# A two-layer decoder trunk on one Trainium2 core: the first FFN pair by eight plain products, and the order of the reloads ahead of the down projection

## The chip, the cores and the metric

The kernel runs on one core of one Trainium2 chip. The metric is the device time of one execution in microseconds (us), lower is better. A core has a matrix engine (TensorE, PE in the profile, with its weight loads as PEld), a vector engine (DVE), a scalar engine (ACT), GpSimd (POOL) and a sync engine (SP) that issues most DMAs. Each engine works through its own instruction queue in order, and waits on semaphores for the others.

## The reference

A segment of a decoder over 1040 positions (16 meta tokens and 1024 tokens) of width 1024, all in float32:

```python
for layer in range(2):
    if layer == 0:
        h = h + mixer_rglru_swa(rmsnorm(h, mix_norm_ab), ...)   # recurrent heads and windowed attention
    else:
        h = h + mixer_retention(rmsnorm(h, mix_norm_ret), ...)  # chunkwise retention
    h = h + swiglu(rmsnorm(h, ffn_norm[layer]), w_gu[layer], w_down[layer])
return h[:, 16:]

def swiglu(x, w_gu, w_down):                 # w_gu (1024, 5632), w_down (2816, 1024)
    gate, up = split(x @ w_gu, 2)
    return (silu(gate) * up) @ w_down
```

The change lies in the two FFNs (`swiglu`) and in what leads into them.

## The kernel before, in words

**Numbers as two halves.** Activations lie with the 1024 features on partitions (8 tiles of 128, index `m`) and the positions along the free axis, cut into two halves (`hf` 0 and 1, each 520 positions in layer 0 and 512 in layer 1). An operand of TensorE is a pair of fp32r tiles: `hi` is a rounded copy (ACT), `lo` is the rest (a subtraction). `hilo` (line 767) makes such a pair of an activation (tiles `oh`, `ol`), `part` (line 108) of a weight (tiles `hi`, `lo`). A product of two operands is three matmuls, `mm3` (lines 149 to 151): hi by hi, lo by hi, hi by lo.

**Seven products.** The FFN's big matrix products are done on 2 by 2 blocks: two tiles of output features by two halves of positions, summed over pairs of input tiles. `seven` (line 773) does such a block with seven products in place of eight (`PRODUCTS`, line 742). For that both sides need sums and differences. The weights' four, S1 to S4, are made on POOL by `unit22` (line 125). The activations' four, T1 to T4, are made by `mixed` (line 759):

```python
t1 = b12 - b11;  t2 = b22 - t1;  t3 = b22 - b12;  t4 = b21 - t2
```

Here `b11` and `b21` are tiles 2j and 2j+1 of half 0, `b12` and `b22` the same tiles of half 1. `MOVING` (line 744) lists the seven activation operands of a block, B11, B21, T2, T1, T3, B22 and T4. `operands` (line 862) makes them for one pair of tiles `j`, with the four differences taken in turn by POOL and DVE and the seven `lo` halves by DVE. There are four such `j`.

**The up phase.** `ffn` (line 790) first runs 11 pairs (`NP`). A pair is one `seven` for the gate columns and one for the up columns, each over the four `j`. Its evacuation applies the norm's scale `R` (made by `ratio`, line 255, from the sums of squares `acc`), Silu, and the product gate by up. Then `mixed` makes the hidden block's own differences, and the seven operands of the pair are written to DRAM (`hd`, on ACT's DMA queue).

**The down phase.** It reads the 16 residual tiles back (`unspill`, line 737, tiles `h<-keep`), and then works in four groups of hidden pairs, (0, 1), (2, 3, 4), (5, 6, 7) and (8, 9, 10). For each group it reloads the seven operands of its pairs (`raw<-hd`, line 847), splits them with `hilo` (the `lo` on POOL), and runs `seven` for each of four blocks `mp` of output tiles, adding into `h` (line 801). The last group hands `h` to `done`.

**What leads into an FFN.** In layer 0 the attention's output projection `out_proj` (line 683) runs for half 0 in the background of attention, and then for half 1, tile by tile: projection, add to `h` (line 694), `normed` (line 746, tile `xp`, on DVE, with the square on ACT and its sum `acc` on POOL, line 756), spill of `h`, and after every second tile `operands`. In layer 1 the retention's last projection (line 1153) does the same, and half 0 is reloaded and normed in `prefetch` (line 1092).

**Buffers.** Pool `sl` has 56 slots of one activation tile each, got by `slot`. Pool `fp` of an FFN has 18 more (`xslot`, `fslot`, tag `xs`). Weight halves `hi` and `lo` have 6 buffers each, raw weight tiles 2, and PSUM has 4 banks of tag `ps` and 4 of tag `ax`.

**Who orders the work.** The code is traced in program order and then scheduled: each instruction gets its place in its engine's queue from a simulated timeline, by priority (program order, with weight loads raised by `tc.high_priority`), as its inputs and a free buffer come available in that simulation. On the chip the queues then run in that order.

Of the kernel before, what the change touches and what calls it, by code (L numbers as in the profile page):

```python
# [22 lines left out]
P = 128  # L23
D = 1024
KD = 8
NM = 16
# [45 lines left out]
def tile_hybrid(ctx: ExitStack, tc, hT, wfm, wqkv, wo0, lruw, pk, qkg, ck, c0, ret_tab, ret_m,  # L72
# [46 lines left out]
    def unit(src, early=True, eng=nc.vector, pool=None):  # L119
        with tc.high_priority() if early else ExitStack():  # L120
            raw = raw_tile()
            nc.sync.dma_start(raw, src)
            return [part(raw[:, i * 512:(i + 1) * 512], 512, eng, pool) for i in range(2)]

# [662 lines left out]

    NP = FT // 2

    def ffn(fp, wgu, wd, xs, R, n, done):  # L790
# [13 lines left out]
        for i in range(NP):  # L804
# [27 lines left out]
            seven(unit22(wgu[i], 512, fp), xs, chunks, blocks(gt))  # L832
            seven(unit22(wgu[NP + i], 512, fp), xs, chunks, blocks(ut))
            m_ = mixed(((ut["11"], ut["12"]), (ut["21"], ut["22"])), n, xslot, (nc.vector,))
# [4 lines left out]
        for m in range(KD):  # L839
            for hf in range(2):  # L840
                h[m][hf] = unspill(m, hf, n, xslot if hf and m >= 4 else None)
        for gi, grp in enumerate(DGROUPS):
            xs = [{} for _ in grp]
            for key in MOVING:
                for j, i in enumerate(grp):
                    raw = xslot("raw")[:, :n]
                    nc.sync.dma_start(raw, hd[i][key])
                    xs[j][key] = hilo(raw, n, slot, nc.gpsimd)
            w = len(grp) * P
            for mp in range(4):  # L850
                h1, h2 = h[2 * mp], h[2 * mp + 1]
# [10 lines left out]
    def operands(j, xp, n, temps, new, eng):  # L862

        m_ = mixed((xp[2 * j], xp[2 * j + 1]), n, temps, (nc.gpsimd, nc.vector))
        return {k: hilo(m_[k], n, new, eng) for k in MOVING}
# [12 lines left out]
    xp = [[None, None] for _ in range(KD)]  # L878
    for m in range(KD):
        xp[m][0] = normed(m, 0, "g1", 520, sc[0], acc[0])  # L880
        spill(m, 0, 0, 520)
    for m in range(KD):
# [3 lines left out]
    xo = []  # L886
    for m in range(KD):
# [4 lines left out]
        if m == 0:  # L892
            Rf = [ratio(acc[0], 520, sc[0], fp), None]
        if m % 2:
            xo.append(operands(m // 2, xp, 520, slot, fslot if m == 5 else slot, nc.vector))
    Rf[1] = ratio(acc[1], 520, sc[1], fp)
# [21 lines left out]
    ffn(fp, wgu0, wd0, xo, Rf, 520, done0)  # L918
# [6 lines left out]
    xo = []  # L925
    acc3 = [None, None]
    with tc.tile_pool(name="m1", bufs=1) as rp:
# [13 lines left out]
        for hf in range(2):  # L941
# [40 lines left out]
            for hd in range(NH):  # L982
# [109 lines left out]
                def prefetch():  # L1092
# [4 lines left out]
                    for kk in range(KD):  # L1097
# [3 lines left out]
                        else:  # L1101
                            xp[kk][0] = normed(kk, 0, "g3", 512, R[0][:, NM:528], acc3[0])

# [42 lines left out]
                def project(u, u_, a, b, yh, yl):  # L1146
                    for j in range(2):
# [8 lines left out]
                        elif b - a == 256 and b == 512:  # L1156
                            xp[m][1] = normed(m, 1, "g3", 512, R[1][:, :512], acc3[1])
                            spill(m, 1, 0, 512)
                            if m in (1, 3, 5):
                                xo.append(operands(m // 2, xp, 512, slot, slot, nc.vector))  # L1160
# [21 lines left out]
    xo.append(operands(3, xp, 512, slot, fslot, nc.vector))  # L1182
# [132 lines left out]
```

## Time and profile before

| what | us |
|---|---|
| time, median of 3 runs | 2770.39 |
| lowest and highest of these | 2769.83 and 2771.3 |
| time of the profiled execution | 2795.01 |
| span of the profiled execution, first to last instruction | 2793.2 |
| PE busy in it | 2654.5 |
| DVE busy | 1653.4 |
| POOL busy | 1381.9 |
| ACT busy | 1142.6 |

The span is what the profile's views divide up, and the profiled execution's own time stands 1.8 us above it. Matmuls are pipelined, so a busy PE is told best by how many matmuls it starts in a stretch. The granted clock of TensorE is given as a share of its full speed (1.00 or 0.5). In a row of the timeline the first two numbers are the start and the duration in us, `x2` means that rows were merged, and the brackets tell how long the engine had been idle before and what ended that. In a row of groups the mean duration in ns stands behind the busy time, and the idle time with its releasers at the end. In a row of a tile three durations in ns are given, the shortest, the median and the longest.

### The profile page before, as it was taken

To read this page: it belongs to the slowest core of one execution; us is meant where nothing else is said; L and a number is where in the kernel's file an instruction comes from. 1 tells how busy PE (TensorE), PEld (TensorE's weight loads), DVE (VectorE), ACT (ScalarE), POOL (GpSimd) and SP (SyncE) were. 2 spreads that over 40 slices of the span, in tenths; PEclk is the share of its full clock that TensorE was granted. 3 is DMA by queue.
4 is the path that set the end of the run, shared out by engine and by line. 5 is a ranking of instruction groups with operands and counts; after the bars stand their busy time and mean duration, and the time that the engine had idled before them with its cause. 6 is when DMAs were issued, how large, how long until landed. Compare 5 with 4: busy or idle time off the path is not lost.

```text
span 2793.2 us, 42909 instructions
## 1 busy us (share of the span) xinstructions
PE 2654.5 (95%) x16079; PEld 2345.8 (84%) x16079; DVE 1653.4 (59%) x2956; ACT 1142.6 (41%) x2350; POOL 1381.9 (49%) x1267
## 2 busy tenths in 40 slices
PE   8979997999999799999999999999967999997999
PEld 7867795999999799988888888888865888885787
DVE  6866458666666577734434454344386565554775
ACT  4654434333333344333434444334443333333342
POOL 3654125554555677733234243343365554555885
PEclk9989698999999899999999999999988999998999
DMA  4001032223222744222121242222231233326442
GB/s 154 32 16 37 29 137 72 84 97 114 96 95 85 262 132 134 94 74 76 69 83 64 80 143 70 91 76 76 83 113 46 102 103 105 113 76 228 152 148 90
DMA packets 111073, 274.59 MB, mean 98 GB/s; under 512 B 13520, under 2 KB 13776, under 8 KB 110864
## 3 DMA queue, kind: packets, MB, share of 16 engines
q1 hardware_dynamic: 87840, 228.86, 24.3%
q10 hardware_dynamic: 22464, 41.14, 3.9%
q8 instruction: 126, 2.06, 0.3%
q0 software_dynamic: 560, 1.85, 0.2%
q14 instruction: 83, 0.68, 0.1%
HBM read 216.37 MB, written 55.43 MB: 97 GB/s over the span
## 4 chain that ended last, share of the span: by engine, by line
PE 88%; DVE 5%; POOL 2%; ACT 2%; issue 2%; DMA 1%; SPq 0%; ACTq 0%; POOLq 0%; DVEq 0%
PE ps L149 19%; PE ps L150 19%; PE ps L151 19%; PE ax L149 8%; PE ax L150 8%; PE ax L151 8%; PE ps L659 1%; PE ps L626 1%; POOL ol L770 1%; DVE lo L113 1%; DVE ol L770 1%; PE ax L642 1%; DVE qs L280 1%; PE ax L1029 1%; PE ps L625 1%
## 5 line engine op out<-in xcount | busy, mean ns | idle before, releaser
L149 PE MATMUL ps<-oh,hi 128*128 128x260 f32 (+1 forms) x1584 | 509.8, 324 | 64.5 <-ACT oh L769 45.0
L150 PE MATMUL ps<-ol,hi 128*128 128x260 f32 (+1 forms) x1584 | 511.7, 324 | 32.4 <-DVE ol L770 31.3
L151 PE MATMUL ps<-oh,lo 128*128 128x260 f32 (+1 forms) x1584 | 508.7, 323 | 0.7 <-DVE lo L113 0.7
L111 ACT CAST hi<-raw 128x512 fp32r<-128x512 f32 (+2 forms) x468 | 280.2, 602 | 537.9 <-PE ps L150 350.4
L150 PE MATMUL ax<-ol,hi 128*128 128x260 f32 (+1 forms) x1188 | 381.3, 321 | 0.0
L149 PEld LDWEIGHTS ps<-oh,hi 128*128 128x128 f32 x1584 | 301.6, 191 | 92.6 <-ACT oh L769 47.0
L151 PE MATMUL ax<-oh,lo 128*128 128x260 f32 (+1 forms) x1188 | 378.3, 321 | 0.0
L149 PE MATMUL ax<-oh,hi 128*128 128x260 f32 (+1 forms) x1188 | 377.6, 321 | 0.0
L113 DVE TENSOR_TENSOR lo<-S,hi 128x512 fp32r<-128x512 f32 (+2 forms) x304 | 258.9, 854 | 175.4 <-ACT hi L111 171.8
L111 ACT CAST hi<-S 128x512 fp32r<-128x512 f32 (+2 forms) x304 | 170.7, 565 | 468.6 <-PE ps L150 220.8
L150 PEld LDWEIGHTS ps<-ol,hi 128*128 128x128 f32 x1584 | 302.0, 191 | 57.9 <-DVE ol L770 32.4
L113 DVE TENSOR_TENSOR lo<-raw,hi 128x512 fp32r<-128x512 f32 (+2 forms) x340 | 281.8, 830 | 112.7 <-ACT hi L111 108.7
L151 PEld LDWEIGHTS ps<-oh,lo 128*128 128x128 f32 x1584 | 301.2, 191 | 25.3 <-DVE lo L113 1.5
L113 POOL TENSOR_TENSOR lo<-raw,hi 128x512 fp32r<-128x512 f32 x128 | 166.8, 1311 | 263.1 <-ACT hi L111 255.4
L280 POOL TENSOR_TENSOR t<-t,rf 128x520 f32<-128x520 f32 (+1 forms) x154 | 215.5, 1405 | 150.2 <-DVE t L801 124.7
L149 PE MATMUL ps<-xh,hi 128*128 128x512 f32 (+1 forms) x752 | 276.9, 370 | 9.4 <-ACT hi L111 7.1
L150 PE MATMUL ps<-xl,hi 128*128 128x512 f32 (+1 forms) x752 | 275.0, 366 | 0.8 <-DVE xl L199 0.6
L151 PE MATMUL ps<-xh,lo 128*128 128x512 f32 (+1 forms) x752 | 272.0, 363 | 0.0
L149 PEld LDWEIGHTS ax<-oh,hi 128*128 128x128 f32 x1188 | 225.1, 190 | 18.1
L150 PEld LDWEIGHTS ax<-ol,hi 128*128 128x128 f32 x1188 | 224.7, 189 | 17.8 <-POOL ol L770 0.3
L151 PEld LDWEIGHTS ax<-oh,lo 128*128 128x128 f32 x1188 | 224.5, 189 | 17.5 <-DVE lo L113 0.2
L770 POOL TENSOR_TENSOR ol<-raw,oh 128x520 fp32r<-128x520 f32 (+1 forms) x154 | 222.3, 1476 | 33.4 <-ACT oh L769 12.1
(319 smaller groups left out, 5832.3 us busy)
## 6 DMA issues: line engine op xcount, KB each, us to landing
raw<-in_wr_dram SPq DMA_DIRECT2D x64, 512.0 KB, 3.2
rb<-in_wgu_dram SPq DMA_DIRECT2D x44, 512.0 KB, 3.3
raw<-in_wgu_dram SPq DMA_DIRECT2D x44, 512.0 KB, 3.3
raw<-hd SPq DMA_DIRECT2D x77, 260.0 KB, 3.3
raw<-hd SPq DMA_DIRECT2D x77, 256.0 KB, 3.0
raw<-in_wrv_dram SPq DMA_DIRECT2D x32, 512.0 KB, 3.2
raw<-in_wro_dram SPq DMA_DIRECT2D x32, 512.0 KB, 3.2
hd<-T ACTq DMA_DIRECT2D x44, 260.0 KB, 2.1
```

The source lines that it names most:

```text
L111: nc.scalar.copy(hi, src)
L113: eng.tensor_tensor(out=lo, in0=src, in1=f32(hi), op=ALU.subtract)
L149: nc.tensor.matmul(ps, ah, bh, start=first and i == 0, stop=False, skip_group_check=more)
L150: nc.tensor.matmul(ps, ah, bl, start=False, stop=False, skip_group_check=more)
L151: nc.tensor.matmul(ps, al, bh, start=False, stop=last and i == n - 1, skip_group_check=more)
L280: (eng or nc.vector).tensor_tensor(out=out_, in0=a, in1=b, op=ALU.mult)
L625: nc.tensor.matmul(ps[:n, :wm], k.q[g][:, i, :n], kHf[g][:, k.w0:k.w0 + wm], start=True, stop=False)
L626: nc.tensor.matmul(ps[:n, :wm], k.q[g][gs, i, :n], kLf[gs, k.w0:k.w0 + wm], start=False, stop=True)
L642: nc.tensor.transpose(pt[:, i * P:(i + 1) * P], k.p[g][:, i, off:off + P], ident)
L659: nc.tensor.matmul(k.po[:n, o:o + 64], sb[:, i * P:(i + 1) * P], vt[:, k.b - len(segs) + 1 + j, g * 64:(g + 1) * 64], start=False, stop=i ...
L770: eng.tensor_tensor(out=lo, in0=src, in1=f32(hi), op=ALU.subtract)
L1029: nc.tensor.matmul(ps[:, :P], kf[d][:, c:c + P], qf[d][:, c:c + P], start=d == 0, stop=d == 1)
```

## The change

The first pair of each FFN's up phase is done by `eight`, four blocks of two plain products each, whose operands are the plain tiles B11, B12, B21, B22 and the plain weight blocks A11 to A22 (`unit4`). The order is the two blocks of half 0 first, then the two of half 1. The plain operands are split as soon as each tile is normed (`plain`). The differences T1 to T4 and their halves are made by `mixes`, all on DVE, placed in the program behind the gate product (j = 0, 1) and behind the up product (j = 2, 3) of that pair. The scale of half 1 is made inside the gate's evacuation (`late[0]`). In the down phase the operands of the first group come ahead of the residual tiles, which are reloaded four at a time, and the first pair's `lo` halves in that group are made by DVE. The hidden block's differences move from `xslot` to `slot`.

```diff
+    def unit4(src):
+        with tc.high_priority():
+            u = {}
+            for i in range(2):
+                raw = raw_tile()
+                nc.sync.dma_start(raw, src[i])
+                for j in range(2):
+                    u[f"A{i + 1}{j + 1}"] = part(raw[:, j * 512:(j + 1) * 512], 512)
+        return u
...
+    def eight(u, xs, chunks, evac):
+        for m, c in ((1, 1), (2, 1), (1, 2), (2, 2)):
+            bk = [bank("ps" if m == 1 else "ax") for _ in chunks]
+            for (a, b), ps in zip(chunks, bk):
+                terms = [((u[f"A{m}{k}"][0][:, j * P:(j + 1) * P], u[f"A{m}{k}"][1][:, j * P:(j + 1) * P]),
+                          xterm(x[f"B{k}{c}"], a, b)) for j, x in enumerate(xs) for k in (1, 2)]
+                mm3(ps[:, :b - a], terms)
+            evac(m, c, [ps[:, :b - a] for ps, (a, b) in zip(bk, chunks)])
...
-            seven(unit22(wgu[i], 512, fp), xs, chunks, blocks(gt))
-            seven(unit22(wgu[NP + i], 512, fp), xs, chunks, blocks(ut))
-            m_ = mixed(((ut["11"], ut["12"]), (ut["21"], ut["22"])), n, xslot, (nc.vector,))
+            if i == 0:
+                def gate0(m, c, bk):
+                    if (m, c) == (1, 2):
+                        R.append(late[0]())
+                    t = gt[f"{m}{c}"] = slot("t")[:, :n]
+                    each(mul, t, bk, R[c - 1])
+                    nc.scalar.activation(t, t, AF.Silu)
+                    mul(t, t, R[c - 1], nc.gpsimd)
+                def up0(m, c, bk):
+                    t = ut[f"{m}{c}"] = slot("t")[:, :n]
+                    each(mul, t, bk, gt[f"{m}{c}"])
+                eight(unit4(wgu[0]), xs, chunks, gate0)
+                late[1](0, 1)
+                eight(unit4(wgu[NP]), xs, chunks, up0)
+                late[1](2, 3)
+            else:
+                seven(unit22(wgu[i], 512, fp), xs, chunks, blocks(gt))
+                seven(unit22(wgu[NP + i], 512, fp), xs, chunks, blocks(ut))
+            m_ = mixed(((ut["11"], ut["12"]), (ut["21"], ut["22"])), n, slot, (nc.vector,))
...
-        for m in range(KD):
-            for hf in range(2):
-                h[m][hf] = unspill(m, hf, n, xslot if hf and m >= 4 else None)
+        def residual(mp):
+            for m in (2 * mp, 2 * mp + 1):
+                for hf in range(2):
+                    h[m][hf] = unspill(m, hf, n, xslot if hf and m >= 4 else None)
         for gi, grp in enumerate(DGROUPS):
             xs = [{} for _ in grp]
-            for key in MOVING:
+            for ki, key in enumerate(MOVING):
                 for j, i in enumerate(grp):
                     raw = xslot("raw")[:, :n]
                     nc.sync.dma_start(raw, hd[i][key])
-                    xs[j][key] = hilo(raw, n, slot, nc.gpsimd)
+                    xs[j][key] = hilo(raw, n, slot, nc.gpsimd if gi or j else nc.vector)
+                if gi == 0 and ki == 1:
+                    residual(0)
             w = len(grp) * P
             for mp in range(4):
+                if gi == 0 and mp < 3:
+                    residual(mp + 1)
...
-    def operands(j, xp, n, temps, new, eng):
-        m_ = mixed((xp[2 * j], xp[2 * j + 1]), n, temps, (nc.gpsimd, nc.vector))
-        return {k: hilo(m_[k], n, new, eng) for k in MOVING}
+    def plain(xs, xp, m, hf, n, new, eng):
+        xs[m // 2][f"B{m % 2 + 1}{hf + 1}"] = hilo(xp[m][hf][:, :n], n, new, eng)
+    def mixes(xs, xp, n, new):
+        def run(*js):
+            for j in js:
+                m_ = mixed((xp[2 * j], xp[2 * j + 1]), n, slot, (nc.vector,))
+                for k in ("T2", "T1", "T3", "T4"):
+                    xs[j][k] = hilo(m_[k], n, new(j), nc.vector)
+        return run
...
         xp[m][0] = normed(m, 0, "g1", 520, sc[0], acc[0])
         spill(m, 0, 0, 520)
+        plain(xo, xp, m, 0, 520, slot, nc.vector)
...
-            Rf = [ratio(acc[0], 520, sc[0], fp), None]
-        if m % 2:
-            xo.append(operands(m // 2, xp, 520, slot, fslot if m == 5 else slot, nc.vector))
-    Rf[1] = ratio(acc[1], 520, sc[1], fp)
+            Rf = [ratio(acc[0], 520, sc[0], fp)]
+        plain(xo, xp, m, 1, 520, fslot, nc.vector)
+    late = (lambda: ratio(acc[1], 520, sc[1], fp), mixes(xo, xp, 520, lambda j: fslot if j == 3 else slot))
```

Layer 1 is changed alike: `plain` for half 0 in `prefetch` and for half 1 behind the last projection, both into `slot`, and `late` with `fslot` for j below 2.

More of the change, by code (lines that the diff above doesn't have):

```diff
@@ L786, in seven, with ffn @@
             evac(i, [ps[:, :b - a] for ps, (a, b) in zip(bk[t], chunks)])
+    def eight(u, xs, chunks, evac):
[6 more added lines that the diff above has]
+            evac(m, c, [ps[:, :b - a] for ps, (a, b) in zip(bk, chunks)])
     NP = FT // 2
-    def ffn(fp, wgu, wd, xs, R, n, done):
+    def ffn(fp, wgu, wd, xs, R, n, late, done):
         chunks = ((0, 260), (260, 520)) if n == 520 else ((0, 512),)
@@ L878, in tile_hybrid @@
     xp = [[None, None] for _ in range(KD)]
+    xo = [{} for _ in range(4)]
     for m in range(KD):
@@ L885, in tile_hybrid @@
         nc.gpsimd.tensor_copy(h[m][1][:, 0:8], h8[:, m * 8:m * 8 + 8])
-    xo = []
     for m in range(KD):
@@ L916, in done0 @@
         meta_put(m, xn2[m][0])
-    ffn(fp, wgu0, wd0, xo, Rf, 520, done0)
+    ffn(fp, wgu0, wd0, xo, Rf, 520, late, done0)
     fctx.close()
@@ L924, in tile_hybrid @@
     xp = [[None, None] for _ in range(KD)]
-    xo = []
+    xo = [{} for _ in range(4)]
     acc3 = [None, None]
@@ L1102, in prefetch @@
                             xp[kk][0] = normed(kk, 0, "g3", 512, R[0][:, NM:528], acc3[0])
+                            plain(xo, xp, kk, 0, 512, slot, nc.vector)
                 fill = [(lambda e=e: gate(e)) for e in range(4)]
@@ L1158, in project @@
                             spill(m, 1, 0, 512)
-                            if m in (1, 3, 5):
-                                xo.append(operands(m // 2, xp, 512, slot, slot, nc.vector))
+                            plain(xo, xp, m, 1, 512, slot, nc.vector)
                 def wout(u_, hd=hd):
@@ L1181, in tile_hybrid @@
     fp = ctx.enter_context(tc.tile_pool(name="ffn1", bufs=1))
-    xo.append(operands(3, xp, 512, slot, fslot, nc.vector))
-    Rf = [ratio(acc3[0], 512, R[0][:, NM:528], fp), ratio(acc3[1], 512, R[1][:, :512], fp)]
+    Rf = [ratio(acc3[0], 512, R[0][:, NM:528], fp)]
+    late = (lambda: ratio(acc3[1], 512, R[1][:, :512], fp), mixes(xo, xp, 512, lambda j: fslot if j < 2 else slot))
     def done1(m):
@@ L1187, in done1 @@
             nc.sync.dma_start(out[m, :, hf * 512:(hf + 1) * 512], h[m][hf][:, :512])
-    ffn(fp, wgu1, wd1, xo, Rf, 512, done1)
+    ffn(fp, wgu1, wd1, xo, Rf, 512, late, done1)
 def _constants():
```

## The prediction

> **What bounds the kernel now.** The chain of waits on the profile's page comes first, then the granted clock and the counts of matmuls by stretch, then the waits of TensorE in the stretches that fall behind. The chain that ended last says who sets the end:
>
> ```profile
> PE 88%; DVE 5%; POOL 2%; ACT 2%; issue 2%; DMA 1%; SPq 0%; ACTq 0%; POOLq 0%; DVEq 0%
> ```
>
> TensorE is the bound, except for some 12% of the span. In the middle of the two up phases it never stops:
>
> ```profile
> 492.00:912.00 420.00, 420.00 (x3506) 1.00 0.27 96
> 2132.00:2532.00 400.00, 400.00 (x1727) 1.00 0.28 97
> ```
>
> The count in brackets is matmuls. One costs 420 / 3506 = 0.1198 us at 260 columns (layer 0) and 400 / 1727 = 0.2316 us at 512 (layer 1). With these, each phase's end can be set against what its matmuls need. These are TensorE rows at the seams, first layer 0, then layer 1:
>
> ```profile
> 453.17 0.28 PE L149 MATMUL ps<-oh,hi 128*128 128x260 f32 x1
> ...
> 924.45 0.28 PE L151 MATMUL ps<-oh,lo 128*128 128x260 f32 x1
> ...
> 1172.83 0.28 PE L151 MATMUL ps<-oh,lo 128*128 128x260 f32 x1
> ...
> 2072.78 0.48 PE L149 MATMUL ps<-oh,hi 128*128 128x512 f32 x1
> ...
> 2548.49 0.40 PE L151 MATMUL ps<-oh,lo 128*128 128x512 f32 x1
> ...
> 2789.06 0.39 PE L151 MATMUL ps<-oh,lo 128*128 128x512 f32 x1
> ```
>
> An up phase is 22 `seven`s. In layer 0 that is 22 x 168 = 3696 matmuls, 442.8 us, against 924.6 - 453.2 = 471.4. The 28.6 over include the second `ratio`'s twenty small matmuls, which the change keeps; the same ones of the first `ratio`, at full clock, take 2.4 us:
>
> ```profile
> 415.36 1.07 PE L265 MATMUL ax<-ckt,acc 128*128 128x1 f32 x10
> ...
> 422.51 1.36 PE L274 MATMUL ax<-dg,ckt 128*128 128x128 f32 x10
> ```
>
> So 26 us are lost there. In layer 1: 1848 matmuls, 428.0 us, against 475.9; less 2 for `ratio` and 1.5 for small waits later on, 44 lost. The down phases have 1848 and 924: 221.4 against 248.4 and 214.0 against 240.6, 27 and 26.6 over. I take 25 and 26 of these as standing at their starts. All of it, 121 us, sits at four places, and the waits of TensorE there (total, times, longest) name the releaser; the two rows of each place come in order of the four:
>
> ```profile
> PE ps L149 <- ACT oh L769: 14.0, 1, 14.0
> PE ps L150 <- DVE ol L770: 4.8, 1, 4.8
> ...
> PE ps L150 <- DVE ol L770: 26.4, 2, 14.8
> PE ps L149 <- ACT t L812: 8.6, 1, 8.6
> ...
> PE ps L149 <- ACT oh L769: 12.2, 1, 12.2
> PE ps L149 <- ACT hi L111: 4.9, 1, 4.9
> ...
> PE ps L149 <- ACT oh L769: 15.5, 1, 15.5
> PE ps L149 <- ACT hi L111: 4.4, 1, 4.4
> ```
>
> At the up phases it waits for activation operands; at the down phases for the first reloaded operand, and once more for a weight half. The rest of the loss is the clock. It falls to 0.5 in each idle stretch, so that means of 0.65 to 0.80 stand beside these:
>
> ```profile
> 439.00:490.00 51.00, 30.31 (x154) 26.61 (x153) 42.41 (x53) 18.60 (x36) 26.27 (x17) 0.73 0.15 53
> 2060.00:2118.00 58.00, 19.85 (x126) 16.63 (x125) 53.70 (x60) 24.82 (x46) 41.45 (x25) 0.65 0.23 82
> 924.00:975.00 51.00, 33.30 (x231) 32.58 (x230) 29.91 (x60) 19.88 (x42) 37.14 (x31) 0.80 0.86 290
> 2549.00:2600.00 51.00, 30.34 (x108) 22.97 (x109) 25.66 (x37) 18.84 (x40) 36.14 (x31) 0.77 0.86 298
> ```
>
> In the second row DVE, the third busy time, is busy for 53.7 of 58 us: there it is the bound.
>
> **The eight products.** Eight in place of seven is 24 matmuls more for each product in layer 0 and 12 in layer 1, twice each: 48 x 0.1198 = 5.8 and 24 x 0.2316 = 5.6. They lie on TensorE's path whole: minus 11.3 us.
>
> **The start of the up phases.** The two blocks of half 0 need B11 and B21 alone, which can be made before the projection of half 1 ends, and scale 0, which `ratio` has made by then. They are 96 matmuls, 11.5 us (48 and 11.1 in layer 1). Behind this cover the last tile of half 1 is added, normed and split: in the chain three DVE instructions and a cast. So the first 14.0 and 26.4 us go, as far as DVE keeps up. What is late next is T2 of the fourth `j`, which the third product of pair 1 reads. So I add up DVE's work until then. These are its groups, and POOL's, in layer 1's stretch (mean ns before the second bar):
>
> ```profile
> L764 DVE TENSOR_TENSOR T<-xp,T 128x512 f32<-128x512 f32 x8 | 13.4, 1671 | 3.6 <-POOL T L764 3.5
> L770 DVE TENSOR_TENSOR ol<-xp,oh 128x512 fp32r<-128x512 f32 x12 | 12.9, 1098 | 0.0
> L749 DVE SCALAR_TENSOR_TENSOR xp<-h,pkt,R 128x512 f32<-128x512 f32 x8 | 9.3, 1193 | 0.0
> L1153 DVE TENSOR_TENSOR h<-ps,h 128x256 f32<-128x256 f32 x10 | 4.1, 412 | 0.0
> L756 POOL TENSOR_TENSOR acc<-acc,sq 128x512 f32<-128x512 f32 x7 | 11.1, 1589 | 7.5 <-ACT sq L755 7.4
> ```
>
> and this is how far an instruction's time goes (ns, shortest, median, longest):
>
> ```profile
> L764 POOL TENSOR_TENSOR T<-xp,xp x16: 1254/1714/1769, 418.2 to 2115.1; 128x520 f32<-128x520 f32 x8, 128x512 f32<-128x512 f32 x8
> L764 DVE TENSOR_TENSOR T<-xp,T x16: 689/1656/1847, 422.3 to 2115.7; 128x520 f32<-128x520 f32 x8, 128x512 f32<-128x512 f32 x8
> L770 DVE TENSOR_TENSOR ol<-T,oh x32: 675/684/1769, 427.4 to 2120.9; 128x520 fp32r<-128x520 f32 x16, 128x512 fp32r<-128x512 f32 x16
> ```
>
> A DVE instruction takes 0.69 us alone and 1.66 beside POOL. The change takes T's eight differences off POOL, so most of the mixing should stand nearer 0.69; POOL still has the squares, the gate's scale and pair 1's S tiles, some twenty instructions. I take 0.9 us for each mixing instruction, with 0.69 and 1.66 as ends. Up to the fourth T2 there are 29 (eight for each of three `j`, then four differences and one half), and four more for the hidden block's own T. Weight halves and evacuations:
>
> ```profile
> L113 DVE TENSOR_TENSOR lo<-raw,hi 128x512 fp32r<-128x512 f32 (+2 forms) x340 | 281.8, 830 | 112.7 <-ACT hi L111 108.7 <-PE ps L150 1.7
> L280 DVE TENSOR_TENSOR t<-ps,rf 128x260 f32<-128x260 f32 x22 | 9.3, 425 | 9.3 <-PE ps L151 9.3
> L280 DVE TENSOR_TENSOR t<-ps,rf 128x512 f32<-128x512 f32 x11 | 7.6, 691 | 9.1 <-PE ps L151 9.1
> ```
>
> Layer 1, from about 2058: adds 4.1, xp 9.3, eight halves of half 1 at 1.10 are 8.8, fifteen weight halves at 0.83 (gate, up, pair 1's gate) 12.5, two scales' some fourteen short instructions 4.5 (an estimate, under 0.69 each), eight evacuations 5.5, the 33 at 0.9 are 29.7: 74.4, so until 2132. TensorE needs the fourth T2 at 2072.8 + 192 x 0.2316 + 2 = 2119, and two products and nine matmuls on, 7.6 us, 2127. That is 5.5 us of stall; with the clock behind it I keep 9. At 0.69 none is left, at 1.66 it is 25 more, 34 with 9 for that and the clock. Layer 0, from 453: last tile 3, eleven weight halves 9.1, a scale 2.3, sixteen evacuations 6.8, 29.7: 51, so 504, against 453.2 + 384 x 0.1198 + 2.4 + 8.0 = 509.6. No stall by the sum; I keep 4 for the waits between cast and half, and at 1.66 it would be 20, 23 with the clock. Gains: 26 - 4 = 22 and 44 - 9 = 35.
>
> The Trainium skill, SBUF — State Buffer, Who interferes with whom, says that a DVE instruction with two SBUF inputs and a GpSimd one that reads SBUF exclude each other for the whole instruction, whoever comes first. By it each of the twenty POOL instructions would hold DVE up by its 1.25 us, 25 us in all. The trace shows 1656 - 689 = 0.97 us for one, and the sum holds some 20; by the rule it would come out about 5 us later, at 2696.
>
> The second scale's chain (DVE, TensorE, POOL, DVE, TensorE, ACT) comes inside the gate, where the block of A21 and A22 can run meanwhile, 5.7 us. TensorE's small matmuls stand in its queue wherever the simulation put them, and the rest of the pair waits behind them if POOL's last square is late; nothing to 3 us, within what I kept.
>
> In layer 1, eight more halves go into the end of the retention, 8 x 0.69 = 5.5 us to 8 x 1.66 = 13.3 of DVE. TensorE still has gates and projections there. I take 2 us, with 0 and 13 as ends. In layer 0 the same eight fall under attention's end and the projection, and cost nothing as long as that covers them; bare, the same 5.5 to 13.3.
>
> **The start of the down phases.** SP's queue and POOL's, layer 0, then SP's in layer 1:
>
> ```profile
> 914.54 16.64 SPq L739 DMA_DIRECT2D h<-keep  x16
> 931.27 11.49 SPq L847 DMA_DIRECT2D raw<-hd  x18
> ...
> 937.00 23.53 POOL L770 TENSOR_TENSOR ol<-raw,oh 128x520 fp32r<-128x520 f32 x17 [9.30 <-DMA raw<-hd]
> ...
> 2537.10 20.89 SPq L739 DMA_DIRECT2D h<-keep  x16
> 2558.33 11.67 SPq L847 DMA_DIRECT2D raw<-hd  x18
> ```
>
> The residual was in the queue 10 us before the up phase ended, and the operands stood behind it until 931 and 2558. With the order turned, four operands take 4 x 11.49 / 18 = 2.6 us to issue from 914.5. Landing (3.3 us on the page) and split (a cast on ACT, taken at 0.69 like a DVE pass of that size, then 0.69 on DVE or 23.53 / 17 = 1.4 on POOL) make it about 922.5, ahead of 924.6:
>
> ```profile
> raw<-hd SPq DMA_DIRECT2D x77, 260.0 KB, 3.3
> ```
>
> All fourteen and the first four residual tiles are 18 issues, 11.5 us; the last lands by 930, and the seventh product of the first block comes six times 12 x 0.1198 on, at 933. The later residual tiles queue behind these, ahead of the second group's operands, which have 40 us. So 12.2 and 15.5 us go, with their clock. The second wait, 4.9 and 4.4 for a weight half, was behind POOL's row of 17 halves; POOL has seven fewer, but the third block comes earlier by as much. I leave that stall with 3 us of clock, 8 each, so 25 - 8 = 17 and 26 - 8 = 18. Ends: 0 and the whole 25 and 26.
>
> **The sum.** 22 + 35 + 17 + 18 - 11.3 - 2 = 79. From the profiled 2795.0 that is 2716. The median is 2770.4, 0.9% shorter; I take the same 79 off it: **2691**. With the residues of the up phases (13), the 2 of the retention and half of the down phases' (8) at nothing it would be 2668.
>
> **The rivals.**
>
> DVE takes TensorE's waits over: the mixing goes at 1.66 us throughout. Then the stalls are 23 and 34 in place of 4 and 9: 44 us less, 2735. For it stands that all sixteen `T<-xp,T` had a median of 1656; against it that POOL made T just then.
>
> The down phases begin as late as now, because the operands' 18 `xs` buffers (two free, the rest under operands of the up phase) come free only at its end: 35 less, 2726. Against it: T2, T1 and T3 of one or two `j` are done with before the last product.
>
> The change doesn't do what it says: the plain operands of half 0 find no slot (16 of them beside 16 of attention's output, 16 xp and h) until the projection ends, so both up phases start as late as now. Left are 35 - 11 - 2 = 22: 2748.
>
> Slower: the mixing runs behind pair 0, not beside it. At layer 0's projection end 16 + 16 + 16 slots and three more are held, 51 of 56, and one `j` wants twelve. If it got none until pair 0's temporaries go, 29 instructions at 1.66, 48 us and 6 of clock, would stand in TensorE's way in each layer: 108 in place of 13, 2786, slower by 16. It decides from 46 us a layer, 1.4 us an instruction. Against it: the 16 slots of attention's output come free at 453, and pair 0 has 46 us left then.
>
> **How the numbers follow.** A measurement of this kernel can tell 0.2%, 5.5 us, from no change. Forecast 0.75; DVE 0.10; down phases 0.06; half 0 late 0.03; mixing behind 0.06, of which 0.04 slower and 0.02 no change. That is 0.94 faster, 0.02 the same, 0.04 slower. The range: 2668 at the low end, as above, and up to 2745, which holds DVE's 2735 and the down phases' 2726 and leaves out the last two.
>
> **What would show it.** Right: TensorE's matmuls go over from line 694's projection to `eight` without a gap, no `ACT oh` wait of 14 or 26 us, DVE full through pair 0 with the mixing's median near 0.7, a stall of some us at pair 1's third product in layer 1, `raw<-hd` issued ahead of `h<-keep`, granted clock near 1.00 at the four seams. Wrong: waits on `DVE ol` over 15 us in pair 1, or `raw<-hd` issued after 924.

## The result and the profile after

| | us | ratio to before, 95% interval |
|---|---|---|
| before, median of 4 runs | 2770.74 | |
| after, median of 4 runs | 2720.88 (2718.7 to 2725.17) | 0.9822 [0.9805, 0.9839] |
| predicted | 2691 (2668 to 2745) | |

The change makes the kernel 49.9 us faster, of the 79 that the prediction summed up. The profiled execution after took 2719.58 us, close to its median; that of before, 2795.01, lies 24.3 above the median of its kernel. The same stretch of attention shows why, first in the windows of before, then of after (span, PE busy and matmuls, PEld, DVE, ACT, POOL, granted clock, DMA share, GB/s):

```profile
285.00:340.00 55.00, 55.00 (x229) 43.22 (x230) 24.59 (x85) 22.65 (x77) 10.07 (x29) 0.60 0.03 8
```

```profile
285.00:340.00 55.00, 55.00 (x367) 45.01 (x365) 33.18 (x113) 29.28 (x98) 9.44 (x28) 1.00 0.09 30
```

In that one execution of before TensorE ran this stretch of attention at a clock of 0.60, and the FFN began 23.5 us late (453.17 against 429.63). The change has no part in it (e2 below, with the same attention, ran there at 1.00), so the two profiles are compared phase by phase and not by their spans. The phases end here at the last evacuation of an up phase and at the last matmul of a down phase:

| kernel | time | up 0 | down 0 | retention and up 1 | down 1 |
|---|---|---|---|---|---|
| before | 2770.7 | 472.6 | 247.1 | 1377.3 | 238.9 |
| after | 2720.9 | 455.4 | 241.3 | 1358.1 | 229.0 |
| gain | 49.9 | 17.2 | 5.8 | 19.2 | 9.9 |

The four gains sum to 52.1. The third column can be cut once more, at the first matmul of layer 1's up phase (2072.78 before, 2030.13 after): the retention takes 899.9 and 903.9, the up phase 477.4 and 454.2. The chain that ended last, on the page of after:

```profile
PE 53%; DVE 3%; POOL 1%; ACT 1%; issue 1%; DMA 0%; SPq 0%; DVEq 0%; ACTq 0%; POOLq 0%
```

Its shares sum to 59 and not to 100, so the 53 can't be set against the 88 of before. The windows are the better measure. The four seams, same columns as above:

```profile
429.63:480.63 51.00, 51.00 (x426) 50.81 (x425) 30.23 (x57) 16.33 (x29) 15.67 (x12) 1.00 0.14 48
2012.00:2070.00 58.00, 55.11 (x317) 47.01 (x317) 44.28 (x64) 22.36 (x39) 33.10 (x22) 1.00 0.29 100
2070.00:2120.00 50.00, 43.15 (x169) 33.35 (x168) 42.05 (x56) 20.03 (x35) 19.39 (x14) 0.93 0.24 85
884.00:935.00 51.00, 40.49 (x293) 38.99 (x294) 42.07 (x82) 23.44 (x51) 32.17 (x28) 0.90 0.81 283
2484.00:2535.00 51.00, 42.06 (x162) 31.77 (x161) 45.20 (x62) 26.47 (x56) 40.19 (x33) 0.93 0.83 283
```

The start of the up phase in layer 0 is closed: 51.00 of 51 us at clock 1.00, where before had 30.31 at 0.73. In layer 1 TensorE runs on into the phase, and a smaller hole stands 60 us later. At the starts of the down phases PE is still idle for 10.5 and 8.9 of 51 us. TensorE's waits at the same places (total, times, longest), in the order of the kernel:

```profile
PE ps L162 <- DVE lo L113: 2.0, 1, 2.0
PE ps L160 <- ACT t L833: 1.1, 1, 1.1
...
PE ps L160 <- ACT oh L780: 6.4, 1, 6.4
PE ps L160 <- DVE h L822: 2.0, 1, 2.0
...
PE ps L162 <- DVE lo L113: 3.2, 1, 3.2
PE ax L162 <- DVE lo L113: 1.8, 1, 1.8
...
PE ps L160 <- ACT oh L780: 5.8, 2, 3.4
```

The waits on activation operands of 14.0 and 26.4 at the up phases are gone. Those on the first reloaded operand, 12.2 and 15.5, are smaller, not gone. Why, the queues of SP and ACT at the start of down 0 tell, in the trace of after (start, duration, in brackets the idle time before it and its releaser; SPq and ACTq are transfers that SP and ACT issue):

```profile
872.42 1.67 SPq L888 DMA_DIRECT2D raw<-hd  x2
...
875.28 7.50 SPq L888 DMA_DIRECT2D raw<-hd  x10
882.94 4.90 SPq L750 DMA_DIRECT2D h<-keep  x4
...
888.36 0.33 ACTq L877 DMA_DIRECT2D hd<-t  x1
889.34 0.33 ACTq L877 DMA_DIRECT2D hd<-T  x1
889.71 2.21 ACT L780 CAST oh<-raw 128x520 fp32r<-128x520 f32 x4 [5.08 <-DMA h<-keep]
```

The raw operands were requested ahead of the residual tiles, as meant. But the first cast ran only at 889.71, 6 us after the up phase's last matmul had begun (883.71), and the releaser named is a transfer that it does not read. Its operand had long landed. Two `xs` buffers were free early, and the first two of the fourteen raw loads were issued at 485.89 and 512.24 and landed by 489.88 and 514.82; the other twelve start at 872.42, and the first of these landed at 875.30. Ahead of the cast in ACT's queue stand the last pair's writes of the hidden block. In the compiled queue, in this order, each write waits for two semaphores:

```
911 L877 DMA hd<-T 128x520 [waits DMAHW4,DVE]
912 L877 DMA hd<-T 128x520 [waits DMAHW6,DVE]
913 L877 DMA hd<-t 128x520 [waits DMAHW0,DVE]
914 L877 DMA hd<-T 128x520 [waits DMAHW1,DVE]
915 L780 CAST oh<-raw 128x520 [waits DMAHW3]
```

DVE's is for the data. The other is one of eight counters on which all the transfers of SP and ACT are booked in turn, so a write is issued only when the transfer before it on its counter has landed. The trace has the counter of each transfer and its landing, and the four writes follow these landings within 0.1 us:

| write issued | counter | transfer before it on that counter | landed |
|---|---|---|---|
| 884.90 | DMAHW4 | `raw<-hd`, issued 880.36 | 884.83 |
| 886.41 | DMAHW6 | `raw<-hd`, issued 881.37 | 886.34 |
| 888.36 | DMAHW0 | `raw<-hd`, issued 882.38 | 888.29 |
| 889.34 | DMAHW1 | `h<-keep`, issued 882.94 | 889.26 |

The Trainium skill (DMA: Bandwidth & Descriptors, Anatomy of one DMA — SWDGE (gpsimd) path) says that DMA engines don't wait on semaphores, and that a wait is done by the sequencer that issues the DMA. That section is on transfers issued by GpSimd. The trace agrees for ACT's: its casts, behind the writes, are held for 5.08 us.

### The profile page after: what moved, and what is told of

Read it like the earlier page. It is cut to its first block, busy times and chain, and to the rows that moved or that the text cites. A ratio compares the mean times of both kernels' runs of the same rounds, so it can differ in the third digit from the quotient of the medians.

```text
span 2717.5 us, 43025 instructions
## 1 busy us (share of the span) xinstructions
PE 2639.5 (97%) x16151; PEld 2331.9 (86%) x16151; DVE 1650.9 (61%) x2976; ACT 1131.8 (42%) x2328; POOL 1305.2 (48%) x1215
## 4 chain that ended last, share of the span: by engine, by line
PE 53%; DVE 3%; POOL 1%; ACT 1%; issue 1%; DMA 0%; SPq 0%; DVEq 0%; ACTq 0%; POOLq 0%
PE ps L161 13%; PE ps L160 13%; PE ps L162 13%; PE ax L160 4%; PE ax L161 4%; PE ax L162 4%; DVE lo L113 1%; PE ax L1081 1%; PE ax L186 1%; DVE xp L760 1%; PE ax L1135 0%; POOL ol L781 0%; DVE ol L781 0%; DVE T L775 0%; PE ax L1096 0%
## 5 line engine op out<-in xcount | busy, mean ns | idle before, releaser
L160 PE MATMUL ps<-oh,hi 128*128 128x260 f32 (+1 forms) x1584 | 506.2, 322 | 19.4 <-ACT oh L780 13.8
L162 PE MATMUL ps<-oh,lo 128*128 128x260 f32 (+1 forms) x1584 | 506.7, 321 | 10.5 <-DVE lo L113 10.4
L160 PE MATMUL ax<-oh,hi 128*128 128x260 f32 (+1 forms) x1212 | 388.0, 322 | 2.0 <-ACT hi L111 0.8
L162 PE MATMUL ax<-oh,lo 128*128 128x260 f32 (+1 forms) x1212 | 387.0, 321 | 2.6 <-DVE lo L113 2.6
L161 PE MATMUL ax<-ol,hi 128*128 128x260 f32 (+1 forms) x1212 | 389.0, 321 | 0.4 <-DVE ol L781 0.4
L111 ACT CAST hi<-S 128x512 fp32r<-128x512 f32 (+2 forms) x288 | 161.2, 562 | 427.8 <-PE ps L161 186.8
L781 POOL TENSOR_TENSOR ol<-raw,oh 128x520 fp32r<-128x520 f32 (+1 forms) x140 | 204.9, 1491 | 26.0 <-ACT oh L780 13.1
```

Source lines behind the costliest of these rows:

```text
L111: nc.scalar.copy(hi, src)
L160: nc.tensor.matmul(ps, ah, bh, start=first and i == 0, stop=False, skip_group_check=more)
L161: nc.tensor.matmul(ps, ah, bl, start=False, stop=False, skip_group_check=more)
L162: nc.tensor.matmul(ps, al, bh, start=False, stop=last and i == n - 1, skip_group_check=more)
L781: eng.tensor_tensor(out=lo, in0=src, in1=f32(hi), op=ALU.subtract)
```

## The experiments

The forecast gain was 79 us and the measured one 49.9. Three theories say where the missing 29 us went, most of it in the down phases. **Queue:** the casts stand behind the last pair's writes on ACT. **Buffers:** when the raw loads start is set by the 18 `xs` buffers and not by the order in the code. **DMA:** the 16 DMA engines are full there, in slices of after,

```profile
883.00:888.00 5.00, 0.99 (x9) 0.78 (x7) 3.34 (x7) 0.41 (x1) 1.24 (x2) 0.98 0.99 309
888.00:893.00 5.00, 2.61 (x10) 2.38 (x11) 2.07 (x2) 2.21 (x4) 2.06 (x2) 0.50 1.05 405
893.00:898.00 5.00, 4.25 (x27) 3.82 (x26) 3.15 (x4) 4.05 (x9) 3.40 (x3) 0.83 1.03 365
```

(last three columns: clock, DMA share, GB/s), and bytes are the bound. In the up phase of layer 1, where TensorE still waits for DVE, the question is whether DVE is the bound. All ratios are to the kernel before.

| kernel | median | ratio, interval | up 0 | down 0 | retention and up 1 | down 1 |
|---|---|---|---|---|---|---|
| e1_up_only | 2719.7 | 0.9797 [0.9759, 0.9835] | 455.5 | 242.5 | 1354.8 | 230.2 |
| e2_down_only | 2746.75 | 0.9892 [0.9854, 0.993] | 472.6 | 234.8 | 1379.2 | 226.2 |
| e3_writes_behind_casts | 2721.72 | 0.9811 [0.9765, 0.9857] | 455.3 | 239.7 | 1355.0 | 232.2 |
| e6_halves_pool | 2719.05 | 0.9795 [0.9753, 0.9837] | 457.0 | 241.3 | 1359.8 | 225.5 |
| e7_t_in_slots | 2756.52 | 0.9932 [0.9909, 0.9956] | 471.7 | 239.5 | 1379.5 | 231.7 |
| e8_order_only | 2755.83 | 0.9931 [0.9907, 0.9955] | 472.2 | 243.7 | 1382.7 | 226.9 |
| e9_half_residual | 2713.55 | 0.9775 [0.9743, 0.9808] | 456.8 | 245.0 | 1351.4 | 226.7 |
| e10_early_freed | 2707.17 | 0.9766 [0.9724, 0.9809] | 460.0 | 233.3 | 1356.8 | 225.0 |
| e11_early_and_behind | 2726.19 | 0.9861 [0.9817, 0.9904] | 459.5 | 240.9 | 1355.7 | 234.8 |
| e12_mix_first | 2701.19 | 0.974 [0.9713, 0.9767] | 459.8 | 234.0 | 1349.6 | 224.8 |
| e5_mix_alt | 2720.26 | 0.9809 [0.9781, 0.9838] | 460.2 | 241.7 | 1362.6 | 224.1 |
| e13_writes_on_sp | 2704.13 | 0.9762 [0.9748, 0.9775] | 459.4 | 235.0 | 1349.3 | 225.0 |

A phase comes from one execution. Where kernels have the same code in it, it scatters: down 0 by under 1 us (241.3, 241.3, 241.7 in after, e6, e5), down 1 by 5 (229.0, 225.5, 224.1), the long middle by 3 to 5 (1354.8 to 1358.1 in after, e1, e3, and 1377.3 to 1382.7 in before, e2, e7, e8).

### One half of the change at a time

```diff
 e1_up_only: after, but
+        for m in range(KD):
+            for hf in range(2):
+                h[m][hf] = unspill(m, hf, n, xslot if hf and m >= 4 else None)
         for gi, grp in enumerate(DGROUPS):
...
-                if gi == 0 and ki == 1:
-                    residual(0)
...
-                if gi == 0 and mp < 3:
-                    residual(mp + 1)
...
-                    xs[j][key] = hilo(raw, n, slot, nc.gpsimd if gi or j else nc.vector)
+                    xs[j][key] = hilo(raw, n, slot, nc.gpsimd)
 e2_down_only: before, with after's down phase and after's T of the hidden block in slots
```

> The up phases as changed (eight products first, plain operands early, mixing beside them), the down phases in the old order: all sixteen residual tiles first, POOL making every low part. By the trace of the changed kernel the up phases bring 17 and 18 us: 2770.5 - 35 = 2735. By the prediction's sums they bring 22 + 35 - 11 - 2 = 44: 2727. If the two parts need each other (the old down order keeps its waits of 12 and 15 us on a first operand whatever the up phases do), the down phases last 248 and 241 us as before; if they shrink here as well, part of the gain that I give to the new order came from the up phases.

> The up phases as before, the down phases as changed. By the trace of the changed kernel the down phases bring 6 and 11 us: 2770.5 - 17 = 2753. By the prediction 17 + 18 = 35: 2735. With the theory that casts of the first operands stand behind the last pair's writes on ACT's queue, the wait on ACT oh at both starts is again some 3 to 6 us and not 0. Attention's code is that of the kernel before: if its TensorE clock is 0.5 for some 50 us here too, the half clock belongs to that code; if it is near 1, it came by chance in one execution and says nothing of the change.

The parts don't add: 53 us alone and 26 alone, 50 together. e2 leaves the up phase where it was (472.6) and takes 12.3 and 12.7 off the down phases, more than the whole change does. e1 keeps almost all of after's gain in the down phases though its code has the old order. Its SP queue in the trace shows why:

```profile
872.69 2.14 SPq L750 DMA_DIRECT2D h<-keep  x2
...
875.55 11.06 SPq L886 DMA_DIRECT2D raw<-hd  x13
887.56 9.61 SPq L750 DMA_DIRECT2D h<-keep  x12
```

Thirteen raw loads went ahead of twelve residual tiles all the same. The scheduler places a load when a buffer for it is free, and e1 still has the one word that frees the `xs` buffers: T of the hidden block goes into `slot`. In e2 attention, the old code, ran at a full clock (its up phase began at 428.34), so the clock of 0.60 above is not that code's own.

### Buffers or order

```diff
 e7_t_in_slots: before, but
-            m_ = mixed(((ut["11"], ut["12"]), (ut["21"], ut["22"])), n, xslot, (nc.vector,))
+            m_ = mixed(((ut["11"], ut["12"]), (ut["21"], ut["22"])), n, slot, (nc.vector,))
 e8_order_only: before, with after's down phase; T stays in xslot
```

> The kernel before with one word changed: the four temporaries T of each hidden block come from the 56 slots and no longer from the 18 xs buffers, into which the raw operands of the down phases are loaded. The order in the code stays: all residual tiles first. Theory (buffers, not the order in the code, decide when the raw loads start: with the up phases as changed and the old order in the code, SP issued 13 of the first 14 raw loads ahead of 12 residual tiles all the same): the down phases fall from 247 and 239 to about 242 and 230, 14 us: 2757. Rival (the order in the code decides): the down phases stay at 247 and 239, 2771.

> The kernel before with the down phases' new order (residual tiles behind the first two keys, the first pair's low parts on DVE), T staying in the xs buffers. Theory (buffers decide): the raw loads stand ahead of the residual tiles in SP's queue, but wait for xs buffers that the last hidden blocks hold until they are written; down phases of 240 to 247 and 232 to 239, 2757 to 2771. Rival (the order decides): 235 and 226 as with the whole down part of the change, 2746.

Each alone brings 15.4 and 16.0 us, together (e2) 25.9. One word about a buffer is worth as much as the whole turned order. The two SP queues, e7's first:

```profile
892.12 9.44 SPq L847 DMA_DIRECT2D raw<-hd  x8
901.62 10.89 SPq L739 DMA_DIRECT2D h<-keep  x12
```

```profile
888.24 17.96 SPq L849 DMA_DIRECT2D raw<-hd  x13
906.25 0.91 SPq L739 DMA_DIRECT2D h<-keep  x2
```

e7's code asks for the residual first and gets the raw loads first. Its loads wait for buffers: the one at 895.00 had its counter free at 892.98 and then waited for TensorE, which still read what lay in the buffer. e8's code asks for the raw loads first, and its thirteen take 17.96 us to issue. What they wait for last in the trace is not a buffer but a counter: the third goes at 896.27, behind a write of ACT's that landed at 896.21, the fourth to sixth at 900.33, 901.14 and 901.80, behind writes that landed at 900.27, 901.07 and 901.73. That T in `xs` is what makes e8 slower than e2 is shown by the one word between them; by which path it does so is not.

### Moving the writes on ACT's queue

```diff
 e3_writes_behind_casts: after, but
-                nc.scalar.dma_start(hd[i][key], m_[key])
+                if i < NP - 1:
+                    nc.scalar.dma_start(hd[i][key], m_[key])
...
+                if gi == 0 and ki == 3:
+                    with tc.issue_after(cast[0]):
+                        for k_ in MOVING:
+                            nc.scalar.dma_start(hd[NP - 1][k_], m_[k_])
```

Here `cast[0]` is the latest cast that `hilo` made, and `tc.issue_after` puts what follows behind it in ACT's queue.

> The changed kernel with the last pair's seven writes of the hidden block put behind the casts of group 0's first four keys on ACT's queue. Theory (the first cast ran at 889.7 only because those writes, ahead of it in the queue, waited for earlier transfers): the waits on ACT oh of 6.4 in layer 0 and 3.4 + 2.4 in layer 1 go, with some 5 us of clock in layer 0: 12 to 17 us, about 2706. Rival 1 (DVE is the bound there, full from 900 to 910): the waits come back as DVE h or DVE lo a few us later, 3 us or less gained, 2718. Rival 2 (the casts wait for their own loads): no change, 2721.

The first cast came at 880.82, before the up phase's last evacuation, as the queue theory says, and the time did not move (2721.7). What was behind the wait took its place: in down 1 PE waited on `DVE ol` for 6.2 us in place of `ACT oh`'s 5.8. So the wait was rightly named, and its price was not its length.

### Loads in time, fewer loads

After keeps in `xs` the operands that the last product pair reads late (half 1's B22, and T up to T4 of one `j`), so the twelve raw loads that did not find a buffer early start 12.6 us before the last evacuation (872.42 to 885.01), against 18.7 for ten in e2 (882.24 to 900.98). The first of the twelve had its counter free at 869.21 and waited for TensorE, that is for a buffer, until 872.42. e10 changes which operands lie there, e9 leaves half of the residual out.

```diff
 e10_early_freed: after, but
-        plain(xo, xp, m, 0, 520, slot, nc.vector)                     # layer 0, half 0
+        plain(xo, xp, m, 0, 520, fslot, nc.vector)
-        plain(xo, xp, m, 1, 520, fslot, nc.vector)                    # layer 0, half 1
+        plain(xo, xp, m, 1, 520, slot, nc.vector)
-    mixes(xo, xp, 520, lambda j: fslot if j == 3 else slot)           # layer 0
+    mixes(xo, xp, 520, lambda k: slot)
-    mixes(xo, xp, 512, lambda j: fslot if j < 2 else slot)            # layer 1
+    mixes(xo, xp, 512, lambda k: fslot if k in ("T2", "T1") else slot)
 e9_half_residual: after, but
-                    h[m][hf] = unspill(m, hf, n, xslot if hf and m >= 4 else None)
+                    h[m][hf] = unspill(m, hf, n) if m < 4 else h[m - 4][hf]
```

> The changed kernel with other activation operands in the xs buffers, those that the last product pair is done with first: in layer 0 the half-0 operands B11 and B21 (read by products 1 and 2) in place of half 1's, in layer 1 T2 and T1 of all four j (products 3 and 4) in place of the four T of two j. Theory (the 16 DMA engines are full, 0.99 to 1.05, from 883 to 920, so what is not loaded by the up phase's end is late): the raw loads start some 5 us earlier, PE's waits on ACT oh shrink, the down phases go from 241 and 229 to about 235 and 224: 2710. Rival 1 (the casts stand behind the last pair's writes in ACT's queue anyway): no change, 2721. Rival 2 (slots become short and the mixing waits): slower by 3 to 10 in the up phases, 2724 to 2731.

> The changed kernel with only eight of the sixteen residual tiles loaded in each layer: tiles 4 to 7 of the model dimension are left out and use those of tiles 0 to 3 in their place. That takes 8 x 260 KB off each down phase's start. Theory (the DMA engines bound the start of the down phases): 2.1 MB at 400 GB/s, 5.3 us less in each: 2710. Rival (queues and the chain of cast, split and evacuation bound it): 2 us or less in each, 2717 or more.

e10 is 13.7 us faster than after. Down 0 falls to 233.3, outside the scatter; down 1, 225.0, lies within it, so for layer 1 the gain is not shown. Its SP queue and its first wait:

```profile
868.20 2.70 SPq L888 DMA_DIRECT2D raw<-hd  x6
...
871.81 3.08 SPq L888 DMA_DIRECT2D raw<-hd  x6
875.46 1.00 SPq L750 DMA_DIRECT2D h<-keep  x2
```

```profile
PE ps L160 <- ACT oh L780: 2.7, 1, 2.7
```

The twelve loads start 19.5 us before the last evacuation (887.65) in place of 12.6, and the wait of 6.4 is 2.7. The rival about slots shows too: up 0 is some 4 us longer.

e9 speaks against bytes as the bound in layer 0: with eight loads fewer down 0 is 3.7 us longer. Raw loads took the residual's place in front of the writes, and the cast came as late as in after:

```profile
889.61 2.21 ACT L780 CAST oh<-raw 128x520 fp32r<-128x520 f32 x4 [4.74 <-DMA raw<-hd]
```

The releaser is another one, the wait is the same. Most of e9's 7.3 us stand in the long middle (1351.4), and there in the retention (896.2 in place of 903.9), whose code the edit leaves alone; that stays open.

### Behind the better loads

```diff
 e11_early_and_behind: e10, with e3's edit
 e12_mix_first: e10, but
+                if n == 512:
+                    late[1](0)
                 eight(unit4(wgu[0]), xs, chunks, gate0)
-                late[1](0, 1)
+                late[1](*((1,) if n == 512 else (0, 1)))
 e13_writes_on_sp: e12, but
-                nc.scalar.dma_start(hd[i][key], m_[key])
+                (nc.scalar if i < NP - 1 else nc.sync).dma_start(hd[i][key], m_[key])
```

> The kernel of e10_early_freed (operands that end early in the xs buffers, 2707) with the last pair's writes of the hidden block behind the casts of the first four keys on ACT's queue. Theory (with the raw loads landed in time, the writes are what still stands ahead of the casts: PE's wait on ACT oh is 2.7 in layer 0 and 3.4 in layer 1): those waits go, 3 to 6 us, about 2702. Rival (as behind the changed kernel, the wait only changes its name, to DVE ol, DVE h and ACT hi): 2705 to 2709.

> The kernel of e10_early_freed with the mixing of the first j in layer 1 put ahead of the first eight products, so that DVE does four differences and four low parts while the first scale is on its way; in the changed kernel DVE waits 4.5 us there for ACT rf and 4.0 before that, then is full from 2070 to 2100. Theory (DVE's work from there to pair 1's third product is the bound in layer 1): 8 x 0.8 = 6 us of it come earlier, PE's waits from 2080 to 2120 shrink by 4 to 7 us with the clock, 2701. Rival (the first scale and the first evacuations come later by as much, and PE waits for a bank): 2707 or some us more.

> The kernel of e12_mix_first (2701) with the last pair's seven writes of the hidden block issued on SP's queue in place of ACT's, where they fall into a stretch in which SP has nothing it can load (879.5 to 890 in the kernel of e10_early_freed). Theory (the writes wait for earlier transfers, and what stands behind them in the same queue waits too: on ACT's it is the casts): PE's waits on ACT oh at the two starts, 2.7 and 3.4, go or halve, the down phases take 230 and 222: 2 to 6 us, 2697. Rival 1 (the next thing is as late, DVE ol behind DVE's T): 2700 to 2702. Rival 2 (now the residual tiles and the second group's operands stand behind the writes on SP's queue): slower, 2705 to 2715.

e11 is 19 us slower than e10, which neither theory had. The writes now stand in the middle of the casts, and they still wait for their counters: those at 899.03, 899.75 and 901.17 follow landings at 898.96, 899.72 and 901.15. ACT's rows of e11:

```profile
896.82 0.35 ACTq L898 DMA_DIRECT2D hd<-t  x1
...
906.58 0.44 ACTq L898 DMA_DIRECT2D hd<-T  x1
907.14 0.41 ACT L111 CAST hi<-S 128x256 fp32r<-128x256 f32 x1 [1.44 <-POOL S L146]
```

From 896.82 to 906.58 the seven writes let only a few weight casts and two of activations through; the next casts come at 907.45, and PE waits 4.4 us for one, until 908.12. How much of the 19 us this makes, no run tells. e13 takes the writes out of ACT's queue altogether. Its down phases are those of e12, 235.0 and 225.0, and its median is 2.9 us above e12's. Its first wait on `ACT oh` falls to 0.9 in down 0 and 0.8 in down 1, and this one comes in down 1, as its first rival had it, with DVE's rows just before it:

```profile
PE ps L161 <- DVE ol L781: 5.5, 1, 5.5
```

```profile
2498.12 1.21 DVE L775 TENSOR_TENSOR T<-t,t 128x512 f32<-128x512 f32 x1
2499.25 1.75 DVE L775 TENSOR_TENSOR T<-t,T 128x512 f32<-128x512 f32 x1
2500.93 2.35 DVE L781 TENSOR_TENSOR ol<-raw,oh 128x512 fp32r<-128x512 f32 x2
```

On DVE the first low parts stand behind the last pair's four T, just as on ACT the casts stood behind the writes of those T. That fits e3 and e13, which freed ACT and gained nothing. It is argued and not shown, as no run here moves DVE's T.

e12 does what its theory says: 6 us less than e10, most of it in the phase that it touches: layer 1's up phase goes from 456.0 to 451.3 (448.4 in e13, which has the same edit). It is the fastest kernel here, 2701.2, some 70 us under before and 20 under after.

### DVE's load in the up phase

```diff
 e6_halves_pool: after, but
-                    u[f"A{i + 1}{j + 1}"] = part(raw[:, j * 512:(j + 1) * 512], 512)
+                    u[f"A{i + 1}{j + 1}"] = part(raw[:, j * 512:(j + 1) * 512], 512, nc.gpsimd)
 e5_mix_alt: after, but
-                m_ = mixed((xp[2 * j], xp[2 * j + 1]), n, slot, (nc.vector,))
+                m_ = mixed((xp[2 * j], xp[2 * j + 1]), n, slot, (nc.gpsimd, nc.vector))
```

> The changed kernel with the low halves of the first pair's eight weight quarters in each layer made on POOL instead of DVE. Theory (DVE is the bound from 2070 to 2100, 10 of 10 us, while POOL is idle): DVE is spared 4 to 8 halves of 0.7 to 1.0 us in layer 1, the waits on DVE lo of 3.2 and 1.8 and their clock go: 4 to 9 us, about 2714. Rival (a DVE instruction beside POOL takes 1.7 in place of 0.7, and a half on POOL is later than one on DVE): the mixing's mean rises from 0.8 to over 1.1, waits move to the weight halves, and the time is the same or up to 8 us longer, 2721 to 2729.

> The changed kernel with the differences T of the mixing going to POOL and DVE in turn, as before the change, in place of DVE alone. Theory (an instruction of DVE takes 0.69 us alone and 1.7 beside POOL): the mixing's mean on DVE rises from 0.8 to about 1.2 and DVE, full from 2070 to 2100 as it is, falls behind by some 5 us net of the eight differences that it is spared; 2722 to 2730. Rival (DVE has too much to do, what is taken off it helps): 2715 to 2719.

Neither moves the time (2719.1, 2720.3). In e5 DVE pays back in longer instructions what it is spared. The mixing of layer 1 in groups (busy, mean ns), after first and then e5:

```profile
L781 DVE TENSOR_TENSOR ol<-T,oh 128x512 fp32r<-128x512 f32 x16 | 12.0, 795 | 0.0
L775 DVE TENSOR_TENSOR T<-xp,T 128x512 f32<-128x512 f32 x8 | 7.6, 951 | 0.0
L775 DVE TENSOR_TENSOR T<-xp,xp 128x512 f32<-128x512 f32 x8 | 6.1, 768 | 0.0
```

```profile
L781 DVE TENSOR_TENSOR ol<-T,oh 128x512 fp32r<-128x512 f32 x16 | 16.3, 1070 | 0.0
L775 DVE TENSOR_TENSOR T<-xp,T 128x512 f32<-128x512 f32 x8 | 8.5, 1059 | 0.1
```

Eight instructions fewer cost DVE 24.8 us in place of 25.7. By phases e5 is longer where its theory has it, 460.1 and 458.1 us in the up phases against 455.4 and 454.2; its last down phase is 4.9 shorter, about that phase's scatter, so the total doesn't show it. e6 does spare DVE something: it is busy for 46.0 of the 70 us from 2050 to 2120 in place of 52.4, and TensorE's longest wait there is still 3.0 us on `DVE lo`. So less work for DVE does not help by itself. When it is done matters more, as DVE's rows of after show, before its full stretch:

```profile
2062.73 0.69 DVE L291 TENSOR_TENSOR t<-ps,rf 128x512 f32<-128x512 f32 x1 [4.53 <-ACT rf L287]
2067.39 0.69 DVE L113 TENSOR_TENSOR lo<-raw,hi 128x512 fp32r<-128x512 f32 x1 [3.97 <-PE ax L161]
```

With these and smaller pauses DVE is idle for 9.7 of the 20 us from 2050 to 2070, while the mixing stands behind them in its queue. It runs from 2068.60 to 2100.99. e12 puts the first `j`'s quarter of it ahead of these waits.

## Why the prediction was right, and where it was short

**Start of the up phases (22 and 35, less 5.8 and 5.6 for the extra products, less 2).** Right in layer 0: 16.2 forecast, 17.2 measured, with waits of 2.0 and 1.1 where 4 were kept. In layer 1 29.4 forecast for the up phase, 23.1 measured (477.4 to 454.2), and 22 to 24 in e1, e3 and e9, which have the same up phase. Of that step the stall was well sized: 6.9 us idle and a clock of 0.93 from 2070 to 2120, some 10 us against the 9 kept. It came in pair 1's third product, as forecast (2091.53, 3.2 us), but on a weight half, `DVE lo`, and not on T2. The sum of DVE's work had left out its waits: DVE was not full through pair 0, and the mixing began only 38.5 us into it. So the rival "the mixing runs behind pair 0, not beside it" was half true in layer 1, though at 0.80 us an instruction; e12, which asks for a quarter of it earlier, shows that its place in the program matters. Some 2 us more go to a term that the prediction had at nothing, TensorE's waits for the last plain operand (0.2 and 1.7, at 2047 and 2049). The rest of the 6 us is open. The retention, for whose end 2 us were taken, went from 899.9 to 903.9, but the same old code there takes 902.6 to 904.8 in e2, e7 and e8, so its cost can't be told from the scatter.

**The mixing's price (0.9 us, ends 0.69 and 1.66).** Right within its ends, and somewhat high: 12.0 + 7.6 + 6.1 = 25.7 us for 32 instructions, 0.80 each. The rival with DVE at 1.66 throughout fell. The Trainium skill's rule (SBUF — State Buffer, Who interferes with whom) that the two engines shut each other out for a whole instruction fits the direction of e5, where the low parts rise from 795 to 1070 ns. The 25 us that the prediction drew from it did not come: 32 x (0.80 - 0.69) is 3.5, with POOL busy for only 7.8 us while the mixing ran. Nor does the prediction's sum hold "some 20" for it, as it says: 0.9 in place of 0.69 is 33 x 0.21 = 7 us in the mixing, and the halves taken at 1.10 and 0.83 hold some 5 more.

**Start of the down phases (17 and 18).** This is the term that failed: 5.8 and 9.9 measured. The failing step reads that "four operands take 4 x 11.49 / 18 = 2.6 us to issue from 914.5" and are ready 2 us ahead of the last matmul. They were requested in time, two of them near 500 and the next from 872.42 on, 11.3 us ahead of the last matmul (883.71), but the first cast ran only at 889.71. The prediction went past SP's and POOL's queues and not past ACT's, which holds the last pair's writes and their waits for counters, nor DVE's, which holds the last pair's T. Its reason for the gain was wrong too. It put the old order down to the code, and e1, e7 and e8 show that buffers decide it at least as much. The rival "down phases begin as late as now, because the operands' 18 `xs` buffers come free only at its end", which had 0.06, was half true: with `xs` buffers that come free earlier, down 0 takes 8 us less (e10), and before to e10 is 13.8 and 13.9, near the 17 and 18. The stall on a weight half, left at 8 us in each layer, is gone in after; it is there in e1 (`ACT hi`, 3.8 and 5.0), so the low parts that moved to DVE or the turned order took it away.

**The rest.** The extra matmuls run at the pace that was taken (426 in 51.00 us, 0.1197 each); their cost was not measured apart. The rival with half 0 late fell: the projection's last matmul starts at 429.39 and the first block's at 429.63. The 24 us of half clock in before's profiled execution were neither seen nor needed, since the same difference was taken off the median. But the profiled time after, 2719.6 against 2716 forecast, looks exact only by luck: 23.5 us that before's profiled execution lost by chance stood against 27 of gain that failed to come.

**Still open.** Down 0 in e12 takes 234.0 us, where 1848 matmuls at 0.1198 need 221.4. How much of the 12.6 could be had is not known; no kernel here moved the last pair's T on DVE and its writes on ACT together.

## What to carry to other kernels

When a transfer is brought forward, go past every queue that its consumer sits in, also for what those queues hold of the stage before: here ACT's writes and DVE's differences of the last pair stood in front of the first cast and the first low part. A write in such a queue can wait for more than its data: here for the transfer before it on a shared counter. Where a scheduler places loads by free buffers, choose what lies in the shared buffers by when it is last read, before turning the order of the code: the one word was worth 15 us alone, better placed operands another 14, and the turned order added nothing behind the new up phases (e1 against after). A wait's length is not its price: take it away, and see what stands right behind it.

## What the runs showed of the hardware

TensorE's granted clock can stand at 0.50 for some 55 us while it is busy without a pause. It did so in before's profiled execution (54.6 us, from 274.6) and again in e13's (54.6 us, from 273.7; 2727.12 us, 23 above that kernel's median):

```profile
285.00:340.00 55.00, 55.00 (x234) 43.22 (x233) 23.94 (x82) 22.73 (x76) 10.07 (x29) 0.61 0.02 6
```

At the same place e2 and after start 365 and 367 matmuls, so the clock shows in the work done and not only in its record. The Trainium skill (TensorE: Matmul & The Clock Gate, Seeing it yourself) knows of the clock sticking for over 50 us, at a quarter; here it was a half. What starts it was not tried.
